# Longer hold of the maxima's transposition and wider groups at the change of token halves in a two-branch attention block

## The chip, the core and the metric

The kernel runs on one core of a Trainium2 chip. A core has five engines with a queue of their own each: TensorE (PE: matrix products; the loading of its weights is shown apart as PEld), VectorE (DVE), ScalarE (ACT), GpSimd (POOL) and SyncE (SP, which here issues nearly all transfers). The metric is the time of one execution on the device in microseconds (us); less is better.

## The reference

One decoder block over 2048 tokens of width 1024, with two token mixers that read the same normalised input `h` and the same input projection:

```python
h = rms_norm(x, norm_gain[l])
proj = h @ w_in[l]
(c_q, c_kv, k_pe, gate_a, q_b, k_b, v_b, gate_b,
 q_i, k_i, w_i, m_a, m_b) = jnp.split(proj, offsets, axis=-1)
...
o_a = mla_attention(q_a, k_a, v_a).reshape(bsz, s_len, MLA_WIDTH) * jax.nn.silu(gate_a)
...
o_b = dsa_attention(q_b, k_b, v_b, q_i, k_i, w_i, k_top).reshape(bsz, s_len, DSA_WIDTH)
o_b = o_b * jax.nn.silu(gate_b)
merged = (jax.nn.sigmoid(m_a + b_merge[l, 0]) * (o_a @ w_branch_mla[l])
          + jax.nn.sigmoid(m_b + b_merge[l, 1]) * (o_b @ w_branch_dsa[l]))
x = x + merged @ w_out[l]
```

`mla_attention` is dense causal attention with 8 heads of 96. `dsa_attention` first scores every visible key with a small indexer (`relu(q_i k_i)` over 8 heads, weighted by `w_i`), keeps the 256 best keys of each query and attends to those alone, with 8 query heads on 2 key heads of 64.

## The kernel before, in words

All products are of 32-bit numbers; where more precision is wanted, each operand is split into a rounded part and a rest ("h" and "l"), and one product becomes three (`mm3`, lines 113 to 115).

**Tokens** (0 to about 340 us). The input is normalised and transposed into `hT`, in two groups `g` of 512 tokens ("token halves" of the 1024 tokens that are in the core's memory at one time): `hT0` and `hT1`, each an h and an l tile of 128 x 8 x 512, 8 being the chunks `kc` of the 1024 features of the model. The first 1024 tokens (`t` below 8) go through first; `hidden` stores their `hT` to memory in `d_h`, since the second 1024 tokens take their place.

**Features** (about 340 to 1085 us). The gates and merge factors are 24 blocks of 128 columns, `c` 0 to 23. `feat` makes one block for one group of 512 tokens: 24 products of 128 x 512 (three for each of 8 chunks), one activation, one store to `d_f`. `FEATURES` (`feature_order`) is the order of the 96 blocks: first the second 1024 tokens (index 0 to 23 of the weights), then, after `load_h` has brought the first 1024 back from `d_h` to the same `hT0` and `hT1`, the same columns again (24 to 47). As a rule a weight is used for group 0 and then for group 1. At the change between the two, two blocks of one group stand together, so that PE has work on one group while the other is reloaded. Weights stand in three buffers (`preload`): a weight is loaded when the weight three before it has been used for the last time; those of the second pass come from `d_w`.

Between the products of the features the kernel weaves three other lanes, so many steps for each slot (`project_features`): the indexer's scores (`scores`: product `z` on PE, `zr` = relu on ACT, sum into `sc` on DVE), the search for each query's threshold (`search`: passes of Sign over all scores on ACT, then selection on DVE and the `bias` on ACT, for two token tiles at a time, 7 pairs), and the preparation of Q and K (`prepare`).

**Attention** (about 1084 to 1960 us). 32 units in the order `UNITS` = (branch, group of 512 queries, pair of heads). A unit has `nk` = 4 (g + 1) key blocks of 128; for each key block and each of its two heads (a **half key block**) PE makes the transposed scores `st` (L646), ACT the exponential `pt` (L674), VectorE or GpSimd add the `pt` up to `acc` (L684), and PE multiplies with the values (`o`, L690). Before a unit may start, it needs the negated maximum of each query's scores: `row_max` makes row-maximum products `ap` on PE (L600, 602), VectorE reduces them to `mx` (L604, 607, 613) and negates to `nm` (L614); `shifts` then transposes `nm` on PE (L623), ACT copies it to `nmT` (L625) and sends it by its own queue into an extra row of Q (L626). These preliminaries of a unit are cut into 8 (g + 1) + 2 **pieces**: the row-maximum products, one piece that is empty of PE work, and last the transposition.

`pipeline` is the planner: after the `st` of every half key block `fill` gives out credit, so that the pieces of the next unit are through `LEAD` half key blocks before the present unit ends, and `take` runs one piece for each whole credit.

On PE the order of the program is the order of the queue. On the other engines and for SyncE's transfers a scheduler orders the instructions by a timeline that it reckons, starting from the order in which they are written. Each engine works through its own queue in order.

Of the kernel before, what the change touches and what calls it, by code (L numbers as in the profile page):

```python
# [9 lines left out]
F32 = mybir.dt.float32  # L10
# [10 lines left out]
P = 128  # L21
S = 2048
D = 1024
NT = S // P
NG = S // 512
KC = D // P
# [14 lines left out]
PREPARE_GAP = 17  # L41
SEARCH_RATE = 1.3
PRIORITY = 200
SEARCH_GAP = 4
INDEX_FIRST = 7
HEADS_FIRST = 10
TAIL = 3
WAIT = 0
LEAD = 6
PT_BUFS = 10  # L50
WINDOW = 8.5
EVALS = 5
# [15 lines left out]
def bcast(ap, n):  # L68
    return bass.AP(tensor=ap.tensor, offset=ap.offset, ap=[[0, P], [1, n]])


class Block:
# [133 lines left out]
    def hidden(self, tok, t):  # L206
        nc = self.nc
        x = tok.tile([P, D], F32, name="x", tag="x", bufs=X_BUFS)
        nc.sync.dma_start(x, self.a["x"][t * P:(t + 1) * P, :])
        if t == 0:  # L210
            nc.sync.dma_start(self.gnorm, bcast(self.a["norm_gain"], D))
        junk = tok.tile([P, D], BF, name="xj", tag="xj")
        ssq = tok.tile([P, 1], F32, name="xs", tag="xs", bufs=2)
        nc.scalar.activation(junk, x, AF.Square, accum_out=ssq)
        rstd = self.rsqrt(tok, ssq, 1, 1.0 / D, "x")
        nc.vector.scalar_tensor_tensor(x, x, rstd, self.gnorm, op0=OP.mult, op1=OP.mult)
        yield
        i, sl = t % 8, slice(t % 4 * P, t % 4 * P + P)
        hi, lo = (m[:, :, sl] for m in self.hT[i // 4])
        for b in range(2):  # L220
            ps = self.pp.tile([P, 4, P], F32, name="tr", tag="tr", bufs=3)
            for k in range(4):
                kc = 4 * b + k
                nc.tensor.transpose(ps[:, k], x[:, kc * P:(kc + 1) * P], self.ident)
            self.split(nc.scalar, hi[:, 4 * b:4 * b + 4], lo[:, 4 * b:4 * b + 4], ps, eng_lo=nc.vector)
        if t < 8:
            for s, m in enumerate((hi, lo)):
                self.move(self.d_h[t][:, s], m)

    def load_w(self, pool, src, n, name, bufs, engines, stage=None):  # L230
        nc = self.nc
# [101 lines left out]


    def load_h(self, g):
        for i in range(4):
            for s in range(2):
                self.move(self.hT[g][s][:, :, i * P:(i + 1) * P], self.d_h[4 * g + i][:, s])

    def feat(self, ev, hf, g, c, w):  # L340
        nc = self.nc
# [63 lines left out]
    def search(self, ip, n, ts, scs):  # L405
# [20 lines left out]
        nt, d = cur[:, :, 0:1], cur[:, :, 1:2]  # L426
# [6 lines left out]
        for e in range(EVALS):  # L433
            for _ in range(SEARCH_GAP):
                yield
            sg = tiny(1, "sg")
            for i, sc in enumerate(scs):
                W = sc.shape[1]
                nc.scalar.activation(junk(W), sc, AF.Sign, bias=nt[:, i], accum_out=sg[:, i])  # L439
            v.scalar_tensor_tensor(d, sg, 0.5, guess[:, :, 1:2], op0=OP.mult, op1=OP.add)  # L440
            ma = ip.tile([P, 2, 2, 1], I32, name="ma", tag="ma", bufs=2)
            v.tensor_scalar(ma[:, :, 0], d, 0.0, None, op0=OP.is_gt)
            v.tensor_scalar(ma[:, :, 1], d, 0.0, None, op0=OP.is_le)
            v.copy_predicated(ends, ma.to_broadcast([P, 2, 2, 2]), cur[:, :, None, :].to_broadcast([P, 2, 2, 2]))
            if e < EVALS - 1:
                v.tensor_tensor(w[:, :, 0:2], hi, lo, op=OP.subtract)
                v.tensor_tensor(w[:, :, 2:3], lo[:, :, 1:2], w[:, :, 0:1], op=OP.mult)
                v.reciprocal(w[:, :, 1:2], w[:, :, 1:2])
                v.tensor_tensor(w[:, :, 2:3], w[:, :, 2:3], w[:, :, 1:2], op=OP.mult)
                v.tensor_tensor(nt, lo[:, :, 0:1], w[:, :, 2:3], op=OP.subtract)  # L450
# [6 lines left out]
        for i, (t, sc) in enumerate(zip(ts, scs)):  # L457
            W = sc.shape[1]
            m8 = ip.tile([P, S], U8, name="m8", tag="m8")[:, :W]
            v.tensor_scalar(m8, sc, th[:, i, 0:1], None, op0=OP.is_gt, op1=OP.add, accum_out=th[:, i, 1:2])  # L460
            yield
            v.copy_predicated(sc, m8, self.sel.to_broadcast([P, W]))
            yield
            for r in range(2):
                v8 = ip.tile([P, 8], F32, name="v8", tag="v8", bufs=2)
                pen = ip.tile([P, 8], F32, name="pen", tag="pen", bufs=2)
                need = ip.tile([P, 1], F32, name="need", tag="need", bufs=2)
                v.max(v8, sc)
                v.tensor_scalar(need, th[:, i, 1:2], -1.0, float(TOPK - 8 * r), op0=OP.mult, op1=OP.add)
                v.tensor_scalar(pen, self.iota8, need, 3.0e38, op0=OP.is_ge, op1=OP.mult)  # L470
                v.tensor_tensor(v8, v8, pen, op=OP.add)
                yield
                v.match_replace(sc, v8, sc, SELECTED)
                yield
            bias = ip.tile([P, S], BF, name="bias", tag="bias", bufs=1)[:, :W]
            nc.scalar.activation(bias, sc, AF.Relu, bias=self.shift)
            nc.sync.dma_start(self.d_m[t][:, :W], bias)
# [249 lines left out]
    def pipeline(self, units, ahead):  # L727
        count = len(units)
        heads, spec, left = [None] * count, [None] * count, [0] * count
        begun, born, clock = 0, [0] * count, [0]  # L730

        def begin(n):
            nonlocal begun
            while begun < count and begun - ahead[begun] <= n:
                m = begun
                heads[m] = units[m]()
                spec[m] = next(heads[m])
                left[m] = 8 * (spec[m]["g"] + 1) + 2
                born[m] = clock[0]
                begun += 1  # L740

        def take(n):
            left[n] -= 1
            next(heads[n])

        begin(-1)
        for n in range(2):
            while left[n]:
                take(n)
                yield  # L750
        values, after = [], []

        def flush(keep=1):
            nonlocal after
            if keep and len(values) < 3:
                return
            while len(values) > keep:
                f, u, j = values.pop(0)
                f(u, j)
            rest = []  # L760
            for age, f, u in after:
                again = (age - 1, f) if age else f(u)
                if again is not None:
                    rest.append((again[0], again[1], u))
            after = rest

        for n in range(count):
            begin(n)
            u = spec[n]
            credit = [0.0]  # L770
            for j in range(u["nk"]):

                def fill(half):
                    slots, pieces, rate = 2 * (u["nk"] - j) - half - LEAD, 0, 0.0
                    for m in range(n + 1, begun):
                        pieces += left[m]
                        rate = max(rate, pieces / max(slots, 1))
                        slots += 2 * spec[m]["nk"]
                    credit[0] += rate
                    for m in range(n + 1, begun):  # L780
                        while left[m] and credit[0] >= 1.0 and clock[0] >= born[m] + WAIT:
                            take(m)
                            credit[0] -= 1.0

                clock[0] += 1
                values.append((self.scores_t(u, j, fill, flush), u, j))
            after.append((AGE, self.finish, u))
            while n + 1 < count and left[n + 1]:
                take(n + 1)
        while values or after:  # L790
            flush(0)
# [169 lines left out]
    def run(self):  # L961
        nc, a = self.nc, self.a
        self.setup()
        self.d_h = [self.dram([P, 2, KC, P], F32, "d_h%d" % t) for t in range(NT // 2)]
        self.d_qi = [self.dram([P, H, 32], F32, "d_qi%d" % t) for t in range(NT)]
        self.d_c = [self.dram([P, 2, 3, P], F32, "d_c%d" % t) for t in range(NT)]
        self.d_qb = [self.dram([P, H, P], F32, "d_qb%d" % t) for t in range(NT)]
# [244 lines left out]
def feature_order():  # L1212
    order = []
    for half in range(2):
        pairs = [(c,) for c in range(24)]
        pairs = pairs[:22] + [(22, 23)] if half == 0 else [(0, 1)] + pairs[2:]
        order += [(half, g, 24 * half + c) for p in pairs for g in range(2) for c in p]
    return order


FEATURES = feature_order()


# [68 lines left out]
```

## Time and profile before

| | |
|---|---|
| time, median of 3 runs | 2342.23 us (2340.57 to 2347.39) |
| profiled execution: time | 2340.68 us |
| profiled execution: span from first to last instruction | 2338.9 us |
| PE busy | 2250.8 us (96%) |
| DVE, POOL, ACT busy | 1417.3, 1193.1, 986.6 us (61, 51, 42%) |
| mean granted TensorE clock | 0.987 of full speed |

The time is what one execution takes; the span is what the trace covers, 1.8 us less. Busy time is the time in which an engine works on an instruction. TensorE's clock has two levels, 2.4 and 1.2 GHz; the granted clock of a stretch is 1.00 when all of it ran at the upper one.

### The profile page before, as it was taken

Reading aid. Unit: us, or ns where it says so; the run is one execution under the profiler, and the core shown is the slowest. Engines: PE = TensorE matmul, PEld = TensorE weight load, DVE = VectorE, ACT = ScalarE, POOL = GpSimd, SP = SyncE. Lnnn points to the kernel's source line nnn. Section 1 sums busy time; section 2 is a strip of 40 time slices with the busy share of each in tenths; the row PEclk is TensorE's granted clock in tenths of the full one; section 3 lists DMA queues with packets and bytes.
Section 4 is the critical chain, followed back from the end, with each engine's and each line's share of the span. In section 5 each row is a group of like instructions: output and inputs, shape, how many; then the busy total and the mean of one; then the engine's idle time right before and its main releaser. Section 6 shows DMA issues by size and latency. Waiting matters only on the chain.

```text
span 2338.9 us, 37920 instructions
## 1 busy us (share of the span) xinstructions
PE 2250.8 (96%) x12882; PEld 1745.5 (75%) x12882; DVE 1417.3 (61%) x3296; ACT 986.6 (42%) x1986; POOL 1193.1 (51%) x1541
## 2 busy tenths in 40 slices
PE   6999999999988999999999999999999999899999
PEld 6999988877776887886555655655655557899988
DVE  6453525588785877856676676677778874322221
ACT  5342325667666677642334434434433443101110
POOL 5875968866754434312344434434774546634432
PEclk9999999999999999999999999999999999999999
DMA  9441345666668655568433322212222102544442
GB/s 311 139 147 54 120 157 166 227 216 196 223 204 262 206 174 180 182 204 240 135 114 102 117 74 64 65 47 71 79 84 82 51 10 78 172 136 141 138 131 77
DMA packets 298100, 326.12 MB, mean 139 GB/s; under 512 B 23408, under 2 KB 228592, under 8 KB 297776
## 3 DMA queue, kind: packets, MB, share of 16 engines
q1 hardware_dynamic: 297392, 323.56, 44.0%
q8 instruction: 101, 1.65, 0.3%
q14 instruction: 95, 0.78, 0.1%
q10 hardware_dynamic: 512, 0.13, 0.0%
HBM read 184.20 MB, written 139.26 MB: 138 GB/s over the span
## 4 chain that ended last, share of the span: by engine, by line
PE 76%; DVE 9%; POOL 6%; issue 3%; ACT 3%; DMA 2%; SPq 0%; DVEq 0%; ACTq 0%; POOLq 0%
PE st L646 18%; PE o L690 11%; PE acc L113 8%; PE acc L115 8%; PE acc L114 8%; PE ap L600 5%; PE ou L115 2%; PE ou L114 2%; PE ou L113 2%; PE br L114 2%; PE br L113 2%; PE br L115 2%; DVE sc L392 2%; PE z L387 2%; ACT junk L439 1%
## 5 line engine op out<-in xcount | busy, mean ns | idle before, releaser
L674 ACT ACTIVATE pt<-st 128x512 f32<-128x512 f32 (+3 forms) x640 | 340.1, 534 | 466.7 <-PE st L646 417.1
L684 POOL TENSOR_TENSOR acc<-acc,pt 128x512 f32<-128x512 f32 (+3 forms) x288 | 328.2, 1140 | 347.8 <-ACT pt L674 337.9
L392 DVE SCALAR_TENSOR_TENSOR sc<-zr,w_i,sc 128x512 f32<-128x512 f32 (+3 forms) x266 | 214.8, 810 | 111.0 <-ACT zr L389 106.9
L646 PE MATMUL st<-Q,K 96*128 96x512 f32 (+3 forms) x960 | 265.8, 384 | 0.6 <-issue 0.6
L604 DVE TENSOR_REDUCE mx<-ap 128x1 f32<-128x512 f32 (+2 forms) x320 | 185.1, 604 | 110.3 <-PE ap L600 63.6
L684 DVE TENSOR_TENSOR acc<-acc,pt 128x512 f32<-128x512 f32 (+3 forms) x288 | 223.4, 776 | 46.5 <-ACT pt L674 43.1
L607 DVE CUSTOM_DVE_ANT_0 mj<-ap,mask 128x512 bf16<-128x512 f32 (+2 forms) x320 | 193.5, 605 | 91.1 <-PE ap L600 81.9
L646 PEld LDWEIGHTS st<-Q,K 96*128 96x128 f32 (+1 forms) x960 | 163.4, 192 | 73.7 <-issue 50.9
L389 ACT ACTIVATE zr<-z 128x512 f32<-128x512 f32 (+3 forms) x304 | 163.0, 545 | 97.1 <-PE z L387 91.5
L113 PE MATMUL acc<-hT1h,wfh 128*128 128x512 f32 x384 | 156.9, 409 | 9.4 <-DMA hT1h<-d_h 7.0
L113 PE MATMUL acc<-hT0h,wfh 128*128 128x512 f32 x384 | 155.2, 404 | 0.7 <-DMA hT0h<-d_h 0.7
L114 PE MATMUL acc<-hT1l,wfh 128*128 128x512 f32 x384 | 151.9, 396 | 1.6 <-DMA d_f<-ev 1.6
L115 PE MATMUL acc<-hT1h,wfl 128*128 128x512 f32 x384 | 152.5, 397 | 0.0
L114 PE MATMUL acc<-hT0l,wfh 128*128 128x512 f32 x384 | 150.9, 393 | 1.1 <-DMA hT0l<-d_h 1.1
L115 PE MATMUL acc<-hT0h,wfl 128*128 128x512 f32 x384 | 151.6, 395 | 0.0
L690 PE MATMUL o<-pt,Vb 128*64 128x512 f32 (+3 forms) x640 | 138.7, 555 | 0.0
L690 PE MATMUL o<-pt,V 128*64 128x512 f32 (+3 forms) x640 | 136.2, 547 | 0.0
L646 PE MATMUL st<-Q,Kd 128*128 128x512 f32 (+3 forms) x320 | 132.9, 416 | 0.0
L106 ACT ACTIVATE mh<-sg 128x256 fp32r<-128x256 f32 x64 | 26.7, 417 | 231.3 <-POOL sg L931 231.2
L929 DVE TENSOR_TENSOR sg<-br,sg 128x256 f32<-128x256 f32 x128 | 53.7, 424 | 115.7 <-PE br L115 102.6
L387 PE MATMUL z<-kT,iqT 128*128 128x512 f32 (+3 forms) x304 | 111.5, 371 | 11.1 <-ACT zr L389 11.1
L646 PE MATMUL st<-Q,Kl 65*128 65x512 f32 (+3 forms) x320 | 117.3, 367 | 0.0
(283 smaller groups left out, 5923.3 us busy)
## 6 DMA issues: line engine op xcount, KB each, us to landing
d_f<-ev SPq DMA_DIRECT2D x96, 256.0 KB
sg<-d_f SPq DMA_DIRECT2D x128, 128.0 KB
wst<-in_w_f SPq DMA_DIRECT2D x96, 128.0 KB
d_w<-wfh SPq DMA_DIRECT2D x24, 512.0 KB
d_w<-wfl SPq DMA_DIRECT2D x24, 512.0 KB
d_q<-phl SPq DMA_DIRECT2D x32, 384.0 KB
d_k<-phl SPq DMA_DIRECT2D x32, 384.0 KB
wfh<-d_w SPq DMA_DIRECT2D x24, 512.0 KB
```

The lines of the kernel that those rows point to most:

```text
L113: mm(ps, lhi, rhi, start=start, stop=False)
L114: mm(ps, lhi, rlo, start=False, stop=False)
L115: mm(ps, llo, rhi, start=False, stop=stop)
L387: nc.tensor.matmul(z[:, :n], qT[:, h], self.kT[:, k0:k0 + n], start=True, stop=True)
L389: nc.scalar.activation(r[:, :n], z[:, :n], AF.Relu)
L392: nc.vector.scalar_tensor_tensor(sc[:, k0:k0 + n], r[:, :n], ws, sc[:, k0:k0 + n], op0=OP.mult, op1=OP.add)
L604: nc.vector.tensor_reduce(mx[:, b:b + 1], ps[:, :n], axis=AX, op=OP.max)
L607: nc.vector.tensor_tensor_reduce(out=junk[:, :n], in0=ps[:, :n], in1=mask[i][:, 512 * b:512 * b + n], scale=1.0, scalar=-3.0e38, op0=OP.su ...
L646: nc.tensor.matmul(banks[hh][:, cols], l, r, start=start and n == 0, stop=stop and n == len(seq) - 1)
L674: nc.scalar.activation(pt[:, n0:], ps[:, n0:], AF.Exp, scale=u["scale"])
L684: eng.tensor_tensor(acc[:, n0:], acc[:, n0:], pt[:, n0:], op=OP.add)
L690: self.nc.tensor.matmul(u["o"][64 * hh:64 * hh + 64, n0:], u["v"](hh, j), pts[hh][:, n0:], start=(j == 0), stop=(j == u["nk"] - 1))
```

## The change

Four edits.

- In `pipeline` the last piece of a unit (`left[m]` = 1, the transposition) is taken only when `SETTLE` = 3 half key blocks have passed since the piece before; the credit meanwhile serves the next unit in line. `LEAD` goes from 6 to 7. The old pair `WAIT` and `clock`, which had no effect at 0, goes.
- At the change of token halves three feature blocks of one group stand together, where two did.
- `d_h` becomes one tensor per group, and `load_h` brings two chunks `kc` of all 512 tokens with one transfer, where it brought one token tile of all chunks. There are 8 transfers of 512 KB for each group before and after; rows are 4 KB in place of 512 bytes on the core's side.
- In `search` the pause between evaluations is 5 steps in place of 4, with one more step after each Sign pass, and three more before `bias`. The lane's steps per slot, `SEARCH_RATE`, stay.

```diff
-SEARCH_GAP = 4
+SEARCH_GAP = 5
...
-WAIT = 0
-LEAD = 6
+LEAD = 7
+SETTLE = 3
...
         if t < 8:
             for s, m in enumerate((hi, lo)):
-                self.move(self.d_h[t][:, s], m)
+                self.move(self.d_h[t // 4][:, s, :, sl], m)
...
     def load_h(self, g):
-        for i in range(4):
+        for k in range(0, KC, 2):
             for s in range(2):
-                self.move(self.hT[g][s][:, :, i * P:(i + 1) * P], self.d_h[4 * g + i][:, s])
+                self.move(self.hT[g][s][:, k:k + 2], self.d_h[g][:, s, k:k + 2])
...
                 nc.scalar.activation(junk(W), sc, AF.Sign, bias=nt[:, i], accum_out=sg[:, i])
+                yield
...
                 v.match_replace(sc, v8, sc, SELECTED)
+                yield
+            for _ in range(3):
                 yield
             bias = ip.tile([P, S], BF, name="bias", tag="bias", bufs=1)[:, :W]
...
-        begun, born, clock = 0, [0] * count, [0]
+        begun = 0
+        turn, taken = [0], [0] * count
...
         def take(n):
             left[n] -= 1
+            taken[n] = turn[0]
             next(heads[n])
...
                     credit[0] += rate
+                    turn[0] += 1
                     for m in range(n + 1, begun):
-                        while left[m] and credit[0] >= 1.0 and clock[0] >= born[m] + WAIT:
+                        while left[m] and credit[0] >= 1.0 and (left[m] > 1 or turn[0] >= taken[m] + SETTLE):
                             take(m)
                             credit[0] -= 1.0
...
-        self.d_h = [self.dram([P, 2, KC, P], F32, "d_h%d" % t) for t in range(NT // 2)]
+        self.d_h = [self.dram([P, 2, KC, 512], F32, "d_h%d" % g) for g in range(2)]
...
-        pairs = pairs[:22] + [(22, 23)] if half == 0 else [(0, 1)] + pairs[2:]
+        pairs = pairs[:21] + [(21, 22, 23)] if half == 0 else [(0, 1, 2)] + pairs[3:]
```

What this does to the order of instructions, at three places.

**PE, unit 1 near its end (the pieces are those of unit 2, the third in the list).** Before, the transposition `ap<-ident,nm` stands right behind the `st` products (L646) of the next half key block after the last row-maximum product (L600, L602 with `trib`):

```order
L600 MATMUL ap<-K,Q 128x512
L602 LDWEIGHTS identb
L602 MATMUL ap<-trib,identb 128x128
L646 LDWEIGHTS trib
L646 MATMUL st<-identb,trib 128x128
L646 MATMUL st<-Q,K 128x512 x3
L646 LDWEIGHTS trib
L646 MATMUL st<-identb,trib 128x128
L623 MATMUL ap<-ident,nm 8x128
L646 MATMUL st<-Q,K 128x384 x3
```

Now the row-maximum products around it are those of unit 3, and the values' products (L693) and more half key blocks stand ahead of it (the changed file's lines are 3 higher):

```order
L603 MATMUL ap<-K,Q 128x128
L605 LDWEIGHTS identb
L605 MATMUL ap<-trib,identb 128x128
L649 LDWEIGHTS trib
L649 MATMUL st<-identb,trib 128x128
L693 MATMUL o<-pt,V 64x512 x4
L649 MATMUL st<-Q,K 128x384 x3
L649 LDWEIGHTS trib
L649 MATMUL st<-identb,trib 128x128
L626 MATMUL ap<-ident,nm 8x128
```

The transposition of this unit moved two half key blocks back, and three half key blocks lie between its last row-maximum product and it.

**SyncE, the reload of half 1.** Before, the loads of the next weight (`wfh`, `wfl` from `d_w`) stand ahead of all eight loads of `hT1`, each of one token tile:

```order
L121 DMA wfh<-d_w_389 128x1024
L121 DMA wfl<-d_w_389 128x1024
L121 DMA hT1h<-d_h_111 128x8x128
L353 DMA d_f_3_386<-ev 128x512
L121 DMA hT1l<-d_h_111 128x8x128
L121 DMA hT1h<-d_h_112 128x8x128
```

Now six of the eight loads, each of one pair of chunks, stand ahead of the weight (`pc` and `d_va` are small transfers of `prepare`):

```order
L121 DMA hT1l<-d_h_108 128x1024
L121 DMA hT1h<-d_h_108 128x1024
L121 DMA pc_9481<-d_c_134 128x2x128
L121 DMA hT1l<-d_h_108 128x1024
L121 DMA hT1h<-d_h_108 128x1024
L552 DMA d_va_245<-pva 128x512
L121 DMA hT1l<-d_h_108 128x1024
L121 DMA hT1h<-d_h_108 128x1024
L121 DMA wfh<-d_w_383 128x1024
L121 DMA wfl<-d_w_383 128x1024
```

The first loads of `hT1` moved ahead of the weight, and each of them now waits for PE by itself; before, the first two waited and the others followed.

**ACT, the search of pair 0.** Before, around the first `bias`:

```order
L548 ACTIVATE pva<-acc 128x512
L389 ACTIVATE zr<-z 128x512
L476 ACTIVATE bias<-sc,shift 128x2048
L389 ACTIVATE zr<-z 128x512 x3
L352 ACTIVATE ev<-acc,bm 128x512
```

Now:

```order
L551 ACTIVATE pva<-acc 128x512
L389 ACTIVATE zr<-z 128x512
L479 ACTIVATE bias<-sc,shift 128x2048
L389 ACTIVATE zr<-z 128x512 x3
L352 ACTIVATE ev<-acc,bm 128x512
```

Nothing moved here. On ACT the rows of the search move for pair 3 alone (tiles 12 and 5), whose search lies over the change of halves.

## Rows read from the trace of the kernel before

**Rows 1.** Windows of the feature and the attention stage; columns in the first line.

```profile
core 0: us, PE busy (x) PEld busy (x) DVE busy (x) ACT busy (x) POOL busy (x), PEclk, DMA share, GB/s
340.00:960.00 620.00, 588.09 (x2756) 484.82 (x2756) 448.48 (x884) 405.35 (x768) 352.05 (x421) 0.98 0.63 203
1040.00:1960.00 920.00, 900.80 (x5139) 552.37 (x5137) 648.14 (x1745) 363.63 (x693) 420.95 (x398) 0.99 0.30 88
```

**Rows 2.** Waits of PE, whole span: us in total, times, longest us.

```profile
PE ap L623 <- DVE nm L614: 16.4, 17, 2.2
...
PE z L387 <- ACT zr L389: 11.1, 6, 3.3
...
PE acc L113 <- DMA hT1h<-d_h: 7.0, 1, 7.0
```

**Rows 3.** Timeline of PE at the change of halves: start us, us, instruction [idle before].

```profile
723.13 0.47 PE L113 MATMUL acc<-hT0h,wfh 128*128 128x512 f32 x1 [0.74 <-DMA hT0h<-d_h]
724.70 0.50 PE L114 MATMUL acc<-hT0l,wfh 128*128 128x512 f32 x1 [1.10 <-DMA hT0l<-d_h]
...
740.40 0.40 PE L387 MATMUL z<-kT,iqT 128*128 128x512 f32 x1
747.83 0.77 PE L113 MATMUL acc<-hT1h,wfh 128*128 128x512 f32 x1 [7.03 <-DMA hT1h<-d_h]
750.19 0.77 PE L114 MATMUL acc<-hT1l,wfh 128*128 128x512 f32 x1 [1.59 <-DMA d_f<-ev]
...
754.01 0.40 PE L113 MATMUL acc<-hT1h,wfh 128*128 128x512 f32 x1
754.24 0.40 PE L114 MATMUL acc<-hT1l,wfh 128*128 128x512 f32 x1
```

**Rows 4.** Timeline of PE: last row-maximum product and transposition of unit 2.

```profile
1105.88 0.23 PE L602 MATMUL ap<-trib,identb 128*128 128x128 bf16 x1
...
1109.02 0.37 PE L623 MATMUL ap<-ident,nm 128*8 128x128 f32 x1 [2.03 <-DVE nm L614]
```

**Rows 5.** Timeline of DVE in the same stretch.

```profile
1107.65 1.15 DVE L684 TENSOR_TENSOR acc<-acc,pt 128x512 f32<-128x512 f32 x1
1108.73 0.14 DVE L614 TENSOR_SCALAR nm<-mx 128x1 f32<-128x1 f32 x1
```

**Rows 6.** Windows of 16 us around the four longest waits; columns as rows 1.

```profile
1104.00:1120.00 16.00, 13.97 (x60) 7.90 (x58) 9.54 (x21) 4.41 (x10) 4.79 (x5) 0.79 0.61 166
1396.00:1412.00 16.00, 14.57 (x76) 8.26 (x77) 10.16 (x23) 4.26 (x10) 3.99 (x6) 0.89 0.13 38
1570.00:1586.00 16.00, 13.92 (x73) 8.07 (x74) 11.90 (x25) 4.25 (x10) 4.64 (x6) 0.89 0.30 96
1744.00:1760.00 16.00, 14.27 (x78) 8.14 (x79) 9.46 (x29) 5.69 (x12) 5.55 (x5) 0.89 0.01 1
```

**Rows 7.** Timeline of SyncE: first and last load of half 1.

```profile
727.09 0.68 SPq L121 DMA_DIRECT2D hT1h<-d_h  x1
...
742.61 1.71 SPq L121 DMA_DIRECT2D hT1l<-d_h  x1
```

**Rows 8.** Transfers from 710 to 718 us, and from 722 to 727 us.

```profile
DMA packets 4568, 2.49 MB, mean 312 GB/s; under 512 B 80, under 2 KB 4440, under 8 KB 4568
...
DMA packets 1484, 1.79 MB, mean 357 GB/s; under 512 B 57, under 2 KB 1080, under 8 KB 1484
```

**Rows 9.** Timeline of ACT: the first `bias` of the search.

```profile
515.53 2.00 ACT L476 ACTIVATE bias<-sc,shift 128x2048 bf16<-128x2048 f32 x1 [4.98 <-DVE sc L473]
```

**Rows 10.** Timeline of PE right after it.

```profile
518.07 0.65 PE L387 MATMUL z<-kT,iqT 128*128 128x512 f32 x1 [3.31 <-ACT zr L389]
```

**Rows 11.** Timeline of ACT's queue: the maxima of unit 22 are sent.

```profile
1572.69 0.63 ACTq L626 DMA_DIRECT2D Q<-nmT  x1
```

**Rows 12.** Timeline of SyncE: the next use of the small buffer.

```profile
1574.51 0.32 SPq L723 DMA_DIRECT2D li<-d_l  x1
```

**Rows 13.** Timeline of PE: transposition of unit 30, and the unit's first product.

```profile
1877.97 0.27 PE L623 MATMUL ap<-ident,nm 128*8 128x128 f32 x1 [0.20 <-DVE nm L614]
...
1884.38 0.45 PE L646 MATMUL st<-Q,Kd 128*128 128x512 f32 x1
```

More of the change, by code (lines that the diff above doesn't have):

```diff
@@ L738, in begin @@
                 left[m] = 8 * (spec[m]["g"] + 1) + 2
-                born[m] = clock[0]
                 begun += 1
@@ L779, in fill @@
                     credit[0] += rate
+                    turn[0] += 1
                     for m in range(n + 1, begun):
-                        while left[m] and credit[0] >= 1.0 and clock[0] >= born[m] + WAIT:
+                        while left[m] and credit[0] >= 1.0 and (left[m] > 1 or turn[0] >= taken[m] + SETTLE):
                             take(m)
                             credit[0] -= 1.0
-                clock[0] += 1
                 values.append((self.scores_t(u, j, fill, flush), u, j))
```

## Prediction

> **What bounds the kernel now.** The windows by stage come first [rows 1]: TensorE (PE) is busy for 588.09 of the 620 us of the feature stage and for 900.80 of the 920 us of the attention stage; the next engine, VectorE (DVE), stands at 448.48 and 648.14. So a microsecond is won where PE stops, or where it runs at half its clock, and nowhere else. The list of what PE waits for [rows 2] says where it stops: 16.4 us in 17 waits of the transposition of the maxima (L623) for the negated maxima `nm`, 11.1 us in 6 waits of the indexer's product `z` for ScalarE (ACT), and 7.0 us in one wait for a reloaded token half. Each is then looked up in the timeline: the change of token halves [rows 3], one wait for the maxima from both engines' sides [rows 4, 5], and the clock around the four longest of these waits [rows 6]. The transfers [rows 7, 8], the search on ACT [rows 9, 10] and the landing of the maxima [rows 11 to 13] follow where they are needed.
>
> **The change of halves.** Before, the loads of half 0 begin when its last block ends, and PE has two blocks of half 1 to do meanwhile; then the other way round. The first return costs 0.74 + 1.10 = 1.84 us of waiting [rows 3]. The second is dearer. The product that starts at 740.40 should be followed 0.23 us later, the step from 754.01 to 754.24; the next starts at 747.83. From 740.40 to 754.01 there are eleven steps (ten feature products and one of `z`), worth 11 x 0.23 = 2.53 us at full pace; they take 13.61. The loss is 11.08 us, of it 7.03 + 1.59 waiting and the rest products at half pace. Together 12.9 us.
>
> The reason is in the transfers: the eight loads of half 1 are issued from 727.09 to 742.61 [rows 7] and the last wait ends at 750.19, 23.1 us after the first issue, while the two blocks of half 0 that cover them last 740.40 - 723.13 = 17.3 us. The change gives them three blocks, 1.5 x 17.3 = 25.9 us. It also cuts the loads by pairs of feature chunks in place of token tiles: as the order on SyncE shows, a pair is loaded as soon as the last block has used that pair (the load waits for PE, pair by pair), and the first product of the next block needs one pair and not the whole half. A pair is used and needed at the same place in its block, so each has the whole 25.9 us plus one block less what that pair's products take, some 32 us where 23.1 were taken. Half 0 has the same relief. I take all 12.9 us as saved; the bounds are 0 and 12.9.
>
> What is late next would be the weights: in the new order the load of the third block's weights on SyncE stands behind six of the eight loads of half 1. That is 6 x 0.52 + 0.38 for two small transfers + 1.05 = 4.6 MB, all of it to land within the first two blocks, 17.3 us. In 512-byte rows the queue moved 312 GB/s (4440 - 80 = 4360 of the 4568 packets there have 512 bytes to 2 KB), and 357 GB/s in a stretch where larger packets are mixed in [rows 8]: 14.7 or 12.9 us, a margin of 2.6 or 4.4. The new loads move rows of 4 KB, so I expect the second. The Trainium skill (DMA: Bandwidth & Descriptors, Specifications) says that 512 bytes are enough for the full rate. By that rule the longer rows bring nothing; the margin would be the 2.6 us and the sum the same, and it only raises the chance of the first rival below. The two stretches speak against it, though the second has only 1.79 MB.
>
> The stores of the halves at the start keep their place and their waits on SyncE, in 512-byte pieces as before: nothing.
>
> **The hold of the transposition.** I walked the planner's loop for all 32 units. Before, between the last row-maximum product of a unit and its transposition there pass no half key block (four units), one (most) or two. What PE runs into is seen at 1105.88 to 1109.02 [rows 4, 5]: the last product, about 1.1 us of other products, then 2.03 us of waiting, because VectorE still has a sum `acc` of 1.15 us to finish and ends `nm` at 1108.73 + 0.14 = 1108.87, 2.99 us after the last product. Afterwards three half key blocks pass in every unit that is not in the feature tail. A half key block is 920 / 640 = 1.44 us in the mean, and 1.07 us at the narrow end of a unit (6.41 us for six, [rows 13]); three are 3.2 us at least. The longest lag before is 2.2 us of waiting plus about 1.1 of work, 3.3. So of the 16.4 us about 0.5 stays: 15.9 saved. The bounds are 0 and 16.4.
>
> The waits also cost clock. Around the four longest, the mean granted clock of 16 us is 0.79, 0.89, 0.89 and 0.89 [rows 6], where PE runs at 1.2 GHz in a part of them and at 2.4 in the rest. A stretch at half pace loses (1 - clock) x 16 us: 3.36 + 3 x 1.76 = 8.6 us. PE had stood for about 2 us just before each. Without the wait I take the clock to stay up: 8.6 saved, bounds 0 and 8.6.
>
> What the hold delays is the landing of the shift row of Q. Before, the transposition stands at least six half key blocks ahead of its unit's first product; `LEAD` 7 in place of 6 takes one block back, the hold costs two, and five remain: 5 x 1.07 = 5.3 us. The row's way: the transfer is issued 0.6 us after the transposition, at 1572.69 in one unit [rows 11], and SyncE, which waits for it before it reuses the small buffer, goes on at 1574.51 [rows 12]: 1.8 us. So 2.4 us are needed and 5.3 are there: nothing. Behind the waiting transposition on PE stand the next products, which no longer wait. While it is held, the pieces go to the unit after it; their Q and K are loaded when a buffer comes free, long before.
>
> **The search.** `SEARCH_GAP`, the new yield between the two Sign passes and the three before `bias` change when instructions are written, and the order lists show that for six of seven pairs the order on ACT stays: `bias` [rows 9] still stands ahead of the next `zr`, and it still waits 4.98 us for VectorE while PE waits 3.31 us [rows 10]. So I give nothing for the 11.1 us of `z`. For pair 3 (tiles 12 and 5), whose search overlaps the change of halves, rows do move, and the pause that let VectorE and ACT catch up is gone: between 0 and another wait like that of 3.31 us; I put in 1.
>
> **The sum.** 12.9 + 15.9 + 8.6 - 1 = 36.4 us. The profiled execution took 2340.7 us: 2304.3. The median of the runs, 2342.2, lies 1.5 above it: **2306 us**. With the small bounds (the clock's last dip kept, pair 3 at 0 or 3.3) its own range is 2301 to 2314.
>
> **The rivals.**
> - *The halves or the weights still come late.* Nothing of the 12.9 is saved, PE only stops a block later: 2319. For it: the queue is full through the whole swap, and three blocks also bring a third weight (1 MB) and more stores. Against: 32 us for what took 23.1. Chance 0.10.
> - *The clock is not given back,* since it falls for another reason than these waits: 2306 + 8.6 = 2315. Against: the four dips stand right behind the four longest waits. Chance 0.10.
> - *The maxima stay late:* VectorE, 70% busy, sees the row-maxima of the next unit earlier and puts `nm` further back, so the waits stay, clock too: 2306 + 24.5 = 2330.5. Against: the order on VectorE is much the same. Chance 0.08.
> - *The search does help:* the 11.1 us of `z` go as well, 2295. Against: the order on ACT. Chance 0.05.
> - *Slower: the shift row lands too late.* Each of 30 units would wait at its first product. To lose the 36.4 us, each must wait 1.2 us, so the transfer must take 5.3 + 1.2 - 0.6 = 5.9 us from its issue, where 1.8 was seen; at 8 us it would be 2306 + 30 x 3.3 = 2405. Chance 0.03.
>
> **How the numbers follow.** The forecast has 0.64. The range, 2296 to 2330, takes in the forecast and the first two rivals (0.84) and ends just short of the third and the fourth. About 0.3% (7 us) can be told from no change by such runs: faster by more than that holds for the forecast and the first four rivals if each is no worse than said; some of that I give away for mishaps that add up. Faster 0.92, within 0.05, slower 0.03.
>
> **What would show it.** Right: no wait of L113 or L114 for `hT` over 1 us and no half clock near 750 us; the list of PE's waits without `nm`, or with under 1 us; the attention stage with a granted clock of 1.00 in the four places; the waits of `z` still about 11 us; PE's first `st` of a unit waiting for nothing. Wrong: PE waiting for `wfh` or `hT` at the second return; L623 waiting as before; a new wait of `st` for a transfer at the start of units; `z` gone from the list.

## The result, and the profile after

The changed kernel takes **2308.53 us** (median of four runs, 2308.13 to 2309.72) where the kernel before takes 2342.72; the ratio is 0.9848, 95% interval [0.9833, 0.9863]. The profiled execution took 2308.13 us with a span of 2306.3, so 32.6 us less span than before. In the tables below the *feature stage* runs from the start of the first feature product on PE to that of the last, and the *attention stage* from the first `st` of unit 0 to the first `br` of the merge. Before they took 738.5 and 883.5 us, now 730.8 and 859.8: **-7.7** and **-23.7**; the tokens ahead of them are 1.4 us shorter and what follows is 0.3 us longer. The tokens take 342.8 to 347.2 us in the fourteen profiles of this case, so that 1.4 is not shown to be the change's.

Lines of the attention stage stand three higher in the new file: L623 is now L626, L614 is L617, L646 is L649. First the same two windows as in [rows 1], of the kernel after:

```profile
core 0: us, PE busy (x) PEld busy (x) DVE busy (x) ACT busy (x) POOL busy (x), PEclk, DMA share, GB/s
340.00:960.00 620.00, 596.57 (x2784) 491.71 (x2783) 456.48 (x900) 410.82 (x779) 354.27 (x422) 0.99 0.62 206
1040.00:1960.00 920.00, 914.71 (x5349) 570.11 (x5348) 658.94 (x1760) 367.40 (x710) 443.70 (x424) 1.00 0.31 92
```

PE is now busy for 914.71 of the 920 us of the attention window, at a granted clock of 1.00. What PE still waits for in the whole span, after, in total, times and longest:

```profile
PE z L387 <- ACT zr L389: 12.5, 8, 3.3
...
PE st L649 <- ACT pt L677: 2.0, 2, 1.7
...
PE ap L603 <- DVE mx L607: 1.4, 1, 1.4
PE acc L113 <- ACT ev L350: 1.3, 1, 1.3
...
PE ap L626 <- DVE nm L617: 1.0, 2, 0.5
```

Against [rows 2]: the wait for `nm` went from 16.4 us in 17 places to 1.0 in 2, that for the reloaded half is gone, and that for `zr` went from 11.1 to 12.5. The two returns at the change of halves, PE's timeline after, where [rows 3] had 0.74, 1.10, 7.03 and 1.59 us of waiting:

```profile
724.57 0.28 PE L387 MATMUL z<-kT,iqT 128*128 128x256 f32 x1
724.69 0.39 PE L113 MATMUL acc<-hT0h,wfh 128*128 128x512 f32 x1
...
747.03 0.39 PE L387 MATMUL z<-kT,iqT 128*128 128x512 f32 x1
747.26 0.40 PE L113 MATMUL acc<-hT1h,wfh 128*128 128x512 f32 x1
```

No row has a wait behind it. SyncE in the same stretch issues the third block's weights, at 727.36 and 728.69, between the sixth and the seventh load of half 1 (726.13 and 729.06), as the order lists had said.

The feature stage is only 7.7 us shorter, though the two returns took 12.9 before by the prediction's count. PE stops elsewhere in the stage nearly as it did, but more half clock follows the stops. Windows of 16 us around three stops that both kernels have, before:

```profile
510.00:526.00 16.00, 12.70 (x55) 10.16 (x54) 13.02 (x29) 8.34 (x16) 10.94 (x13) 0.89 0.79 270
643.00:659.00 16.00, 14.05 (x68) 11.57 (x67) 11.75 (x32) 11.88 (x23) 5.14 (x8) 1.00 0.52 171
689.00:705.00 16.00, 13.08 (x67) 11.14 (x66) 8.81 (x16) 8.75 (x17) 5.74 (x6) 1.00 0.82 258
```

The same stops after:

```profile
510.00:526.00 16.00, 12.69 (x48) 10.02 (x47) 12.84 (x28) 7.39 (x14) 11.80 (x12) 0.79 0.83 292
643.00:659.00 16.00, 13.96 (x61) 11.33 (x60) 11.72 (x33) 12.61 (x25) 4.40 (x7) 0.89 0.53 167
689.00:705.00 16.00, 13.05 (x61) 11.24 (x62) 7.87 (x16) 8.39 (x17) 4.33 (x5) 0.89 0.90 304
```

The clock's column goes from 0.89, 1.00, 1.00 to 0.79, 0.89, 0.89: 1.8 us lost before and 6.9 after. At a fourth stop, near 593 us, it went from 0.89 to 1.00, so that the stage lost 3.4 us more at these four.

The queue moves more than in [rows 8]; the transfers after, from 724 to 740 us:

```profile
DMA packets 2334, 6.58 MB, mean 411 GB/s; under 512 B 241, under 2 KB 529, under 8 KB 2333
```

And unit 2, whose transposition waited 2.03 us in [rows 4]. PE's timeline after:

```profile
1099.67 0.23 PE L605 MATMUL ap<-trib,identb 128*128 128x128 bf16 x1
...
1102.46 0.27 PE L626 MATMUL ap<-ident,nm 128*8 128x128 f32 x1
...
1107.62 0.39 PE L649 MATMUL st<-Q,K 97*128 97x512 f32 x1
```

VectorE (DVE) in the same stretch, where [rows 5] had `nm` behind a sum:

```profile
1100.24 0.68 DVE L687 TENSOR_TENSOR acc<-acc,pt 128x512 f32<-128x512 f32 x1
...
1101.36 0.15 DVE L617 TENSOR_SCALAR nm<-mx 128x1 f32<-128x1 f32 x1
```

`nm` ends 1.84 us after the start of the last product (1101.36 + 0.15 - 1099.67), the transposition starts 2.79 us after it, and 5.2 us are left until the unit's own first product at 1107.62, the least of all units. The windows of 16 us at the places of [rows 6] (units 2, 14, 22, 27), after:

```profile
1096.00:1112.00 16.00, 16.00 (x90) 10.13 (x89) 12.85 (x30) 5.87 (x14) 6.08 (x7) 1.00 0.58 162
1380.00:1396.00 16.00, 16.00 (x90) 9.90 (x91) 12.87 (x28) 6.12 (x13) 6.42 (x8) 1.00 0.22 67
1550.00:1566.00 16.00, 14.65 (x80) 9.23 (x78) 13.54 (x29) 5.86 (x12) 5.77 (x7) 1.00 0.51 151
1722.00:1738.00 16.00, 16.00 (x105) 10.58 (x105) 12.32 (x41) 6.72 (x14) 5.98 (x7) 1.00 0.16 47
```

All four at full clock.

### The profile page after: what moved, and what is told of

Read it like the earlier page. It is cut to its first block, busy times and chain, and to the rows that moved or that the text cites. A ratio compares the mean times of both kernels' runs of the same rounds, so it can differ in the third digit from the quotient of the medians.

```text
span 2306.3 us, 37951 instructions
## 1 busy us (share of the span) xinstructions
PE 2237.9 (97%) x12882; PEld 1739.7 (75%) x12882; DVE 1418.4 (61%) x3296; ACT 982.5 (43%) x1986; POOL 1194.9 (52%) x1541
## 5 line engine op out<-in xcount | busy, mean ns | idle before, releaser
L649 PE MATMUL st<-Q,K 96*128 96x512 f32 (+3 forms) x960 | 264.7, 383 | 1.0 <-issue 0.6
L649 PEld LDWEIGHTS st<-Q,K 96*128 96x128 f32 (+1 forms) x960 | 163.0, 191 | 73.6 <-issue 52.3
L693 PE MATMUL o<-pt,V 128*64 128x512 f32 (+3 forms) x640 | 134.5, 541 | 0.0
L693 PE MATMUL o<-pt,Vb 128*64 128x512 f32 (+3 forms) x640 | 134.5, 541 | 0.0
L649 PE MATMUL st<-Q,Kd 128*128 128x512 f32 (+3 forms) x320 | 133.4, 418 | 0.0
L387 PE MATMUL z<-kT,iqT 128*128 128x512 f32 (+3 forms) x304 | 111.6, 371 | 12.5 <-ACT zr L389 12.5
L649 PE MATMUL st<-Q,Kl 65*128 65x512 f32 (+3 forms) x320 | 117.2, 367 | 0.0
```

What stands on the lines that cost most here:

```text
L387: nc.tensor.matmul(z[:, :n], qT[:, h], self.kT[:, k0:k0 + n], start=True, stop=True)
L649: nc.tensor.matmul(banks[hh][:, cols], l, r, start=start and n == 0, stop=stop and n == len(seq) - 1)
L693: self.nc.tensor.matmul(u["o"][64 * hh:64 * hh + 64, n0:], u["v"](hh, j), pts[hh][:, n0:], start=(j == 0), stop=(j == u["nk"] - 1))
```

## The experiments

Twelve kernels were run, each against the kernel before in the same session (its medians there: 2343.55, 2343.32 and 2343.37 us). The ratio's 95% interval stands in brackets; stages are those of one profiled execution.

| kernel | median us | ratio | feature stage | attention stage |
|---|---|---|---|---|
| hold_only | 2322.91 | 0.9913 [0.9896, 0.9930] | 739.1 | 861.6 |
| halves_only | 2331.43 | 0.9947 [0.9929, 0.9965] | 727.9 | 882.6 |
| search_only | 2343.90 | 1.0005 [0.9994, 1.0016] | 741.9 | 882.6 |
| no_hold | 2323.70 | 0.9914 [0.9898, 0.9931] | 731.2 | 875.3 |
| groups_only | 2332.52 | 0.9951 [0.9934, 0.9968] | 733.6 | 881.7 |
| loads_only | 2329.06 | 0.9946 [0.9930, 0.9963] | 727.7 | 880.4 |
| hold_halves | 2307.60 | 0.9852 [0.9836, 0.9868] | 727.3 | 862.3 |
| late_rows | 2379.66 | 1.0149 [1.0130, 1.0167] | 730.7 | 935.0 |
| hold_loads | 2309.27 | 0.9853 [0.9839, 0.9868] | 730.5 | 860.2 |
| bias_vector | 2311.34 | 0.9858 [0.9844, 0.9872] | 729.5 | 861.4 |
| bias_pool | 2346.59 | 1.0013 [1.0005, 1.0022] | 768.9 | 859.0 |
| bias_vector_ohl | 2310.39 | 0.9864 [0.9847, 0.9881] | 728.7 | 860.2 |

**The three parts, each alone.** The edits are those of the diff above, cut to one part each.

hold_only: 

> The kernel before with LEAD 7 and the hold of three half key blocks alone; the change of halves and the search stay as before. Theory (the hold takes the stalls behind nm and the half clock after them, and nothing else): the wait of ap at L623 for nm falls from 16.4 us in 17 to under 2, the attention stage shortens by 23 to 25 us, the hT wait of 7.0 us stays, total 2318 us, ratio 0.990. Rival 1 (the clock is not given back, only the stalls): 2326. Rival 2 (part of the gain in the attention stage comes from the other edits, which shift when this stage begins): under 15 us saved, 2327 or more.

The wait for `nm` fell to 1.0 us in 2, the attention stage by 21.9 us. The theory holds, 1 us short of its 23 to 25, and rival 2 falls; the total, 2322.91, is 5 us above the theory's and 3 below rival 1's, but the stage decides, since stalls alone are 15.4. About 2 us are lost again at 1785 us, where `st` waits 2.4 us for `pt` and the clock dips after it.

halves_only: 

> The kernel before with groups of three feature blocks and the loads of hT by pairs of chunks alone. Theory (the groups and the loads save the 12.9 us at the change of halves, and the 4 us that are missing in the feature stage after the whole change come from the search): 2330 us, ratio 0.9945. Rival (the edit itself gives back 4 us, through the half clock and the waits that it moves elsewhere in the stage): 2334, ratio 0.9965. In both the wait for hT is gone and no window near 750 us shows a clock under 0.95.

The feature stage fell by 10.6 us, 2.3 less than the theory's 12.9, and the waits for `hT` are gone. The median, 2331.43, is 1.4 us above the theory's total; the interval just reaches the rival's 0.9965.

search_only: 

> The kernel before with the search spread over more steps, alone. Theory (ScalarE's order hardly changes, so z waits as before): 2342 us, within 2 us. Rival 1 (it costs the 4 us missing in the feature stage): 2346. Rival 2 (it takes part of the 11.1 us of z): 2336 or less.

No change that the runs can tell. The `z` waits are 12.4 us in 8 places where they were 11.1 in 6.

**Which part of the hold.** no_hold undoes the hold and keeps the earlier start:

```diff
 LEAD = 7
-SETTLE = 3
+SETTLE = 0
```

> The changed kernel with SETTLE 0: LEAD stays 7, so that the transposition is placed up to one half key block behind the last maximum product, as before. Theory (the distance from the last maximum product is what counts, not the earlier start): nm waits of 15 us or more in 15 or more places return, total 2331 us, ratio to the kernel before 0.995. Rival (the earlier start of the pieces by LEAD did it): 2309, as with the whole change.

Neither total came: 2323.70. The waits are back, nearly as the theory had them, but the attention stage is 8.2 us shorter than before. What PE waits for `nm` in no_hold, whole span:

```profile
PE ap L626 <- DVE nm L617: 14.2, 19, 1.2
```

Its window of the attention stage:

```profile
1040.00:1960.00 920.00, 902.00 (x5219) 553.98 (x5218) 645.75 (x1743) 364.01 (x699) 430.58 (x406) 1.00 0.30 88
```

With `LEAD` 7 the pieces meet VectorE's sums at other moments: almost as much waiting (14.2 us for 16.4), in shorter stops (1.2 us at most, where the longest were 2.2), and the granted clock stays at 1.00. So this kernel separates the two terms of the prediction that always came together: 8.2 us came with the clock that is not lost, and the hold itself takes off 875.3 - 859.8 = 15.5 us more, the 13.2 us of `nm` waiting and some 2 besides. The hold with `LEAD` 6 was not run, so what `LEAD` 7 adds to it is open.

**Which part of the change of halves.** groups_only has groups of three blocks and loads by token tiles; loads_only has groups of two and loads by pairs of chunks.

groups_only: 

> The kernel before with groups of three feature blocks at the change of halves alone; hT is still loaded by token tiles of 512-byte rows. Both parts of this edit together shorten the feature stage (first product of features to the last) from 738.6 to 727.9 us. Theory (the third block is 7.6 us of cover, about the 7.0 us wait for hT1h): this wait is under 1 us, stage 730 us, total 2335. Rival (the late loads are a matter of the order in which the rows come: products of a group need all eight transfers before the second chunk): the wait stays above 3 us, stage 735 us or more, total 2340.

loads_only: 

> The kernel before with hT loaded by pairs of chunks alone; groups of two feature blocks as before. Theory (the loads begin 13 us ahead of the product that needs them, a pair of chunks arrives about every 5 us at the rate of before and products use a pair in 1.9 us, so that the last pair is late by 1 to 2 us): the hT waits fall from 8.7 us to 2 or less, stage 731 us, total 2336. Rival (by pairs of chunks the first pair can only be loaded when the last block has read it, so that nothing is won without the third block): waits of 5 us or more, total 2341.

The loads alone do all of it (727.7 us, no wait for `hT` at all), and better than their theory, which left 1 to 2 us at the last pair. With the third block alone the stage is 733.6 us, between theory and rival, and the wait for `hT` is gone there too. What is late in groups_only is another load; its waits of PE from 715 to 770 us:

```profile
PE acc L113 <- DMA wfh<-d_w: 1.3, 1, 1.3
PE acc L113 <- ACT ev L350: 1.2, 1, 1.2
PE acc L115 <- DMA wfl<-d_w: 0.6, 1, 0.6
```

Its window at the first return:

```profile
720.00:736.00 16.00, 14.10 (x64) 11.30 (x63) 5.22 (x14) 7.68 (x14) 4.59 (x5) 0.89 1.03 372
```

These are the weights of the first block behind the return, issued at 715.24 behind the eight loads of half 0: 1.9 us of waiting and 1.8 us of clock. They are late only in this kernel, with short rows and three blocks. The other 2.2 us to loads_only are not shown to come from the change of halves, and the medians, 2332.52 and 2329.06, lie in one another's intervals.

hold_halves leaves out only the search edits, hold_loads the third block too.

hold_halves: 

> The whole change without the search edits. Theory (the search edits cost 3 us of the feature stage, as search_only with 741.9 us against 738.6 and halves_only with 727.9 against the whole change's 730.8 have it): stage 728 us, total 2305.5 us, ratio to the kernel before 0.9835. Rival (the search edits pay for themselves together with the rest, and the 3 us are scatter): 2308.5 or more, 0.985.

hold_loads: 

> The kernel before with the hold (LEAD 7, SETTLE 3) and the loads of hT by pairs of chunks alone: groups of two feature blocks, search as before. Theory (loads_only shortened the feature stage to 727.7 us, as far as both parts of that edit together with 727.9): feature stage 728 us, total 2307.6 us as with hold_halves. Rival (the third block is needed where the stage begins at another moment): hT waits of over 2 us come back, total 2312.

Both give the whole change's time: their intervals lie on one another. The feature stage without the search edits is 727.3 us in one and 730.5 in the other, so the 3 us that I had put on the search in these expectations are not shown to be the search's. What differs between those two profiles is mostly the clock after the same stops. The timeline of PE at one `z` product in hold_loads:

```profile
649.78 0.50 PE L387 MATMUL z<-kT,iqT 128*128 128x512 f32 x1 [1.93 <-ACT zr L389]
```

The window of 16 us around it:

```profile
644.00:660.00 16.00, 14.07 (x62) 11.47 (x61) 11.71 (x33) 12.63 (x26) 4.38 (x7) 0.89 0.52 170
```

The same product in hold_halves:

```profile
648.44 0.51 PE L387 MATMUL z<-kT,iqT 128*128 128x512 f32 x1 [1.96 <-ACT zr L389]
```

And its window:

```profile
642.00:658.00 16.00, 14.04 (x69) 11.54 (x68) 11.75 (x32) 11.98 (x23) 5.04 (x8) 1.00 0.51 174
```

The same stop, of 1.93 and 1.96 us, costs (1 - 0.89) x 16 = 1.8 us of clock in one execution and nothing in the other. A stop of 2.94 us for `phl`, at 695.51 in hold_loads and 692.74 in hold_halves, does the same (0.89 and 1.00 over 16 us); the two make 3.5 us where the stages differ by 3.2.

**How late the shift row may come.** late_rows moves the transposition to the other end:

```diff
-LEAD = 7
-SETTLE = 3
+LEAD = 5
+SETTLE = 6
```

> The whole change with LEAD 5 and SETTLE 6: the transposition of the maxima stands six half key blocks behind the last maximum product, and in about 16 units not one half key block is left before the unit's first product. Theory (the shift row is needed 2.4 us or more after the transposition, and a unit's first st waits for what is missing of that): st waits of 1 to 2 us in 10 or more places behind a transfer into Q or behind nm, several of them with half clock, total 2325 to 2340. Rival (the row lands under other work even then, because the first products of a unit do not read it): 2309.

The mechanism is the theory's, the price more than twice that: the attention stage grew by 75.2 us over the whole change's, where the theory's totals left 16 to 31. Waits of late_rows from 1100 to 2040 us:

```profile
PE st L649 <- DMA Q<-nmT: 37.7, 15, 7.0
PE st L649 <- DMA Q<-d_qb: 5.9, 1, 5.9
...
```

One of them in PE's timeline, behind unit 3's transposition:

```profile
1148.64 0.27 PE L626 MATMUL ap<-ident,nm 128*8 128x128 f32 x1
1151.74 1.19 PE L649 MATMUL st<-Q,K 97*128 97x512 f32 x2 [2.83 <-DMA Q<-nmT]
```

Between the two ScalarE (ACT) copies the maxima and issues their transfer, in its timeline:

```profile
1149.30 0.66 ACTq L629 DMA_DIRECT2D Q<-nmT  x1
```

From the transposition to the product that its row releases: 1151.74 - 1148.64 = 3.1 us, of it 2.4 from the issue of the transfer. The other 31.6 us beyond the two waits are mostly clock: the window from 1040 to 1960 us has 0.96 where the whole change has 1.00. At the longest wait, 6.95 us at unit 22, four loads of the mask, 1.34 MB, were issued in the 3 us ahead of the row's 4 KB, which were issued at 1598.51, and the product started at 1605.11, 7.2 us after its transposition (1597.89). That the mask held the row up is likely, but was not tested.

**Can the rest of the waits go too?** The `z` waits of 3.3 and 3.0 us follow a `bias` for which ACT stands still [rows 9, 10]. Three kernels on top of hold_loads:

```diff
-nc.scalar.activation(bias, sc, AF.Relu, bias=self.shift)
+v.tensor_scalar(bias, sc, -SELECTED / 2, 0.0, op0=OP.add, op1=OP.max)
```

(bias_pool has `nc.gpsimd` for `v`.)

bias_vector: 

> As hold_loads, with the mask's values `bias` made on VectorE, which also makes their input sc, in place of ScalarE. Theory (ScalarE stands still for 5.0 and 6.7 us before two of these, with zr behind them, and the z waits of 3.3 and 3.0 us with half clock after each are its echo): the z waits fall from 11 to 5 us or less, half clock near 517 and 872 us is gone, total 2298. Rival (VectorE carries the sum over heads that zr waits for through its buffers, and the work added there delays it): z waits of 9 us or more in other places, total 2307.

bias_pool: 

> As hold_loads, with `bias` made on GpSimd in place of ScalarE. Theory (any engine but ScalarE will do): total 2298, as with VectorE. Rival (GpSimd then waits for sc with the splits of the feature weights wfh and wfl behind it, and these come late): acc waits of over 2 us for wfl or wfh, total 2305 or more.

bias_vector_ohl: 

> As bias_vector, with the first split of the merge's operand (ohl, at about 1770 us, in the attention stage) made on GpSimd, which makes its input mo, in place of ScalarE and VectorE. Theory (ScalarE stood still for 3.8 us before it, with pt behind, and st's wait of 3.0 us for pt with 6.8 us of half clock is its echo): that wait is gone, attention stage 857 us instead of 862, total 5 us below bias_vector. Rival (the two passes on GpSimd delay the sums acc of pt there, and st waits for pt's buffers instead): no gain, or st and acc waits of 3 us or more.

On VectorE the `z` waits fell as expected, from 11.8 to 5.1 us, but the feature stage only from 730.5 to 729.5 and the time not at all. Other waits came in their place, small ones for several results (all waits of PE in the stage: 21.9 us in hold_loads, 20.8 here). The rival had the kind right and the place wrong. PE's timeline in bias_vector at the dearest of these stops:

```profile
695.16 0.45 PE L583 MATMUL tr<-ident,pqk 128*96 128x128 f32 x1 [4.47 <-DVE phl L109]
```

VectorE's timeline in the same kernel, ahead of it:

```profile
689.98 2.16 DVE L476 TENSOR_SCALAR bias<-sc 128x1792 bf16<-128x1792 f32 x1
...
694.42 0.68 DVE L109 TENSOR_TENSOR phl<-tr,phl 96x512 fp32r<-96x512 f32 x1
```

The mask's 2.16 us stand ahead of the split `phl`, whose wait is 4.47 us where hold_loads has 2.94. Counted from the stage's first product, PE is there 3.5 us earlier than in hold_loads, and the split ends only 2.0 us earlier. On GpSimd the mask is dear, 38 us more feature stage. GpSimd's timeline in bias_pool:

```profile
701.63 7.04 POOL L476 TENSOR_SCALAR bias<-sc 128x1792 bf16<-128x1792 f32 x1
```

VectorE's, in the same stretch:

```profile
702.51 4.36 DVE L392 SCALAR_TENSOR_TENSOR sc<-zr,w_i,sc 128x128 f32<-128x128 f32 x1
...
710.17 0.68 DVE L109 TENSOR_TENSOR phl<-tr,phl 96x512 fp32r<-96x512 f32 x1
```

PE's, right behind:

```profile
710.90 0.45 PE L583 MATMUL tr<-ident,pqk 128*96 128x128 f32 x1 [9.17 <-DVE phl L109]
```

PE waits for the split `phl`, which stands on VectorE behind a sum `sc` of 4.36 us; the median of the 21 sums of that size is 0.35 us. So it is with each of the seven masks of 4.5 us and more: while GpSimd makes one, a VectorE instruction takes 2.6 to 6.7 us whose line and size take 2.2 at most in hold_loads. GpSimd's own next work, `pqk` at 708.75, waits behind the mask too. The total went the rival's way, but not through the weights that it named. bias_vector_ohl took the wait for `pt` at 1770 us away, and the attention stage fell by 1.2 us, not 5: the wait was 2.0 us in this pair, not 3.0, and PE's waits for `nm` and `mx` grew by 1.7 us in its place. No version is measurably faster than the change itself; hold_loads does the same with less.

## Why the prediction was right, step by step

- **The sum.** 36.4 us were predicted and 34.2 measured on the medians, 2308.53 for 2306. The profiled executions, for which the sum was made, differ by 32.6: the attention stage gave 23.7 of 24.5, the feature stage 7.7 of 11.9, and 1.4 came from the tokens, where nothing was forecast. That the medians lie closer is the scatter of the runs, and so luck.
- **The hold** (15.9) and **the clock** (8.6): 24.5 predicted for the attention stage, 23.7 measured. no_hold splits it as 15.5 and 8.2, and hold_only has 21.9 without any other edit. 0.5 us of waiting was to stay, 1.0 did. That the clock is lost through the longest of these waits, and not for another reason, is borne out by no_hold, nearly the same waiting in shorter stops and no dip, and by the others: in the window from 1040 to 1960 us the five kernels with `nm` stops of 2.0 us and more (before, halves_only, search_only, groups_only, loads_only) have a granted clock of 0.99, and all kernels without them, late_rows apart, 1.00.
- **The change of halves** (12.9): 10.6 to 11.2 us (halves_only, hold_halves, loads_only), and less in the whole change, where the feature stage gave 7.7. The waits went as said, the one of 1.59 us too, which the profile puts down to a store (`d_f<-ev`) though its product reads `hT1l`; two things came in their place. PE now runs into a wait of 1.3 us for `ev` (L350) some 10 us later, in every kernel that has lost the wait for `hT`. And stops that were there before, near 517, 649 and 694 us, are followed by a clock dip, or a longer one, in some of these executions; the sum had no term for that, and in the whole change it cost 3.4 us more than before. Step by step: the prediction gave the gain to both edits together. Loads by pairs of chunks are enough, and the third block adds nothing that shows. The reason, that each pair of chunks is loaded as early as it is free and needed as late as its place in the block, is argued from the order of the loads. The third block's weights, which I named as late next, are not late in any kernel; in groups_only the first block's are, by 1.9 us.
- **The rows of 4 KB.** I expected them nearer to 357 than to 312 GB/s; the queue moved 411 from 724 to 740 us, and 360 during the reload of half 0, from 700 to 708 us. The Trainium skill (DMA: Bandwidth & Descriptors, Specifications) puts 512 bytes as enough for the full rate; these traces speak against it for such reloads, 312 GB/s with 512-byte rows in [rows 8] and 360 to 411 with 4 KB, though other traffic is mixed into all these stretches.
- **The search** (-1, 11.1 us of `z` stay): 12.5 us of `z`, so 1.4 more waiting, and search_only's time is 1.0005 of before, [0.9994, 1.0016]. Whether the feature stage pays up to 3 us for it is open: the three kernels with these edits and the new loads have 730.7 to 731.2 us, but hold_loads has 730.5 without them.
- **The landing of the row** ("2.4 us are needed and 5.3 are there"): there are 5.2, and late_rows shows 3.1 needed where little else moves, 7.2 where a mask is loaded at that moment. The step ended right, with less room than it gave; the rival on the slower side is real, and 75 us dear once nothing is left.

## What to carry to other kernels

A wait on TensorE costs its own length, and a longer one often clock behind it; so first break up or take away the longest (here four of 17 stood ahead of every dip in their stage), and read the granted clock right behind each. A result that another engine must finish is best placed a counted amount of work behind its last input, with the same count checked on the far side, where its own reader stands. When a buffer is refilled, cut the transfer in the order in which the old content is used up and the new is needed; moving a waiting instruction to another engine only pays if nothing that TensorE needs stands behind it there, or on an engine that it slows.

## What the runs showed of the hardware

- Nineteen stops of PE of up to 1.2 us for `nm`, and one of 2.5 us for `pt`, left the granted clock at 1.00 (no_hold); of the stops of 1.93 and 1.96 us at the same place shown above one was followed by a dip and one was not, and all four of 1.73 to 2.20 us for `nm` in the kernel before were.
- GpSimd took 7.10 us to add to and clip 128x2048 values from f32 to bf16 (bias_pool), VectorE 1.22 (bias_vector); the 2.16 us above, for 128x1792, are VectorE's slowest. The Trainium skill (GPSIMD Engine Reference, Engine selection) has one-input operations there at roughly the line rate; the masks do not agree with that. Another of GpSimd's one-input operations in the same run, `acc` from `pt` (L682), 128x512 from f32 to f32, took 0.62 us in the mean, 1.2 ns for each element of a row where the mask took 3.5.
- While GpSimd made a mask of 4.5 to 7.1 us, one VectorE instruction each time took 2.6 to 6.7 us (bias_pool), where that line at that size took 2.2 at most in hold_loads; why was not tested.
- A transfer of 4 KB took 2.4 us from its issue to the product that it released in a quiet stretch, and 6.6 us with 1.34 MB of masks issued just ahead of it (late_rows).
